# Latent attention's queries and keys split straight out of PSUM, their rows carried to the operand tiles by DMA

## The chip, the cores and the metric

The kernel runs on one core of one Trainium2 chip. The metric is the device time of one execution in microseconds (us). In the code's names nc.tensor is TensorE (PE in the profile; PEld is its weight load), nc.vector is VectorE (DVE), nc.scalar is ScalarE (ACT), nc.gpsimd is GpSimd (POOL), and nc.sync is SyncE (SP), which here only issues DMAs. PSUM is what PE writes; SBUF is the working memory.

## What is computed

The whole kernel is a decoder block: norm, one wide input projection, an indexed sparse attention (A), a latent attention (B), gates that merge them, an output projection, and a gated MLP with a convolution, on 1024 tokens of 1024 channels. The change touches latent attention, and the last gates ahead of it:

```python
q_b = einsum('bsr,rhd->bshd', c_q, w_uq)        # 8 heads, 64 plain + 32 rotary channels
q_nope, q_rope = q_b[..., :64], apply_rope(q_b[..., 64:])
k_nope = einsum('bsr,rhd->bshd', c_kv, w_uk)    # 64 per head
k_rope = apply_rope(b_kr)                       # 32, one for all heads
sc = (q_nope . k_nope + q_rope . k_rope) * (64 + 32) ** -0.5
p = softmax(where(causal, sc, -inf))
o_b = p . v_b
merged = sigmoid(g_a) * y_a + sigmoid(g_b) * y_b
```

All matrix products are made to nearly fp32 accuracy from three matmuls of split operands: each operand x is a rounded part hi and a rest lo = x - hi, and x.y is hi.hi + hi.lo + lo.hi (`mm3`, L176 to L189, and `scores`, L710).

## The kernel before

**Order of work.** `run` (L236) writes the stages down one after another; a scheduler then gives every engine one instruction list of its own, in which work that is ready on its model of time may stand ahead of work written earlier. An engine runs its list strictly in order. Around the change the text says: `prep_v` (values and the rotary part of the queries, which goes out to DRAM as `qr_d`, L1080), `prep_k(bp0, 0)` (operand tiles of the even heads, memory that had been zeroed by POOL at L1093, rotary rows of the keys at L1100 to L1103), `project(0)`, `operands(st0, 0, 0)`, the gates 14 and the first half of 15 (L323, L324), the first two score blocks, the second half of gate 15 (L331), `prep_k(bp1, 1)` (the odd heads' tiles), and `attn_b`.

**Latent attention** handles the 8 heads as 4 pairs `pr`, of an even head (`par` 0) and an odd one (`par` 1). A pair's queries and keys are projected together: 128 PSUM rows, 64 of each head. The operand tiles `hq[par]`, `hk[par]` hold hi and lo as [128, 1024] each: for an even head rows 0 to 63 are the plain channels, 64 to 95 the rotary ones, 96 to 127 zero; for an odd head the plain channels are rows 64 to 127, the rotary ones 0 to 31.

`project(pr)` (L1105) makes four PSUM tiles of 128x512 (queries and keys, two halves of the tokens), each moved to a fp32 tile `st` of the ring by ACT (L1124). `operands(st, pr, par)` (L1128) then makes, for each of the four pieces, hi by a DVE cast of 64x512 (L1136) and lo by a POOL subtraction (L1137), and copies the query's rotary rows in from `qr_d` by two DMAs on SP (L1144).

`attn_b` (L1197) has 16 steps (pr, par, j), j being the half of the eight query blocks. A step weaves three lists: the scores of its four blocks (`score_b`, matmuls L723 and the causal mask L721 into one of two PSUM tiles; minimum on DVE L1159 or L1161, exp on ACT L1167, reciprocal L1168, and scaling on POOL L1169), the `parts` (transposes L1209, hi on ACT L1218, lo on DVE L1219) and `values` (L1228) of the step before, and extra work: the next pair's `project` in step (pr, 1, 0), its even operands in (pr, 1, 1), and the odd operands in (pr+1, 0, 0). At the end of a step `finish_heads` (L1172) uses two small tiles, fin0 and fin1. All 128x512 PSUM tiles, of the projection too, come from one ring of four (`psA`). The ring `st` in SBUF has three buffers.

## Time and profile before

| | us |
|---|---|
| three timed runs | 1594.61, 1597.29, 1597.31 (median 1597.29) |
| the profiled execution, its whole time | 1594.33 |
| its span, first to last instruction | 1592.5 |
| PE busy | 1507.2 (95%) |
| DVE busy | 1187.3 (75%) |
| POOL busy | 910.5 (57%) |
| ACT busy | 789.4 (50%) |

The rows below come from this one execution; their clock starts at the span's start. A busy share is an average over stages with different limits, and a matmul's recorded length (0.39 us for 512 columns) overlaps the next one's start (0.23 us later). So the reader should go to the stretch of latent attention, about 418 to 590 us, look where PE is idle there, and see in the lists of the other engines what it waited for.

### The profile page before, as it was taken

Reading aid. Unit: us, or ns where it says so; the run is one execution under the profiler, and the core shown is the slowest. Engines: PE = TensorE matmul, PEld = TensorE weight load, DVE = VectorE, ACT = ScalarE, POOL = GpSimd, SP = SyncE. Lnnn points to the kernel's source line nnn. Section 1 sums busy time; section 2 is a strip of 40 time slices with the busy share of each in tenths; the row PEclk is TensorE's granted clock in tenths of the full one; section 3 lists DMA queues with packets and bytes.
Section 4 is the critical chain, followed back from the end, with each engine's and each line's share of the span. In section 5 each row is a group of like instructions: output and inputs, shape, how many; then the busy total and the mean of one; then the engine's idle time right before and its main releaser. Section 6 shows DMA issues by size and latency. Waiting matters only on the chain.

```text
span 1592.5 us, 21976 instructions
## 1 busy us (share of the span) xinstructions
PE 1507.2 (95%) x7586; PEld 1255.6 (79%) x7586; DVE 1187.3 (75%) x1860; ACT 789.4 (50%) x1454; POOL 910.5 (57%) x769
## 2 busy tenths in 40 slices
PE   9989999989899999999999989999999999989996
PEld 7768888867688877998878877888888887767874
DVE  7368999934588888885636668777777766896996
ACT  4545522223377788775434444444444444434445
POOL 4142122411667767654732399777777772487684
PEclk9989999999999999999999999999999999999999
DMA  7331133330300022213762132222222204964343
GB/s 256 108 105 46 54 105 97 111 115 27 106 14 17 14 83 93 76 56 118 238 198 87 53 93 80 80 80 82 81 84 84 85 36 162 329 210 127 126 137 123
DMA packets 74842, 166.25 MB, mean 104 GB/s; under 512 B 9634, under 2 KB 14114, under 8 KB 74722
## 3 DMA queue, kind: packets, MB, share of 16 engines
q1 hardware_dynamic: 62640, 139.59, 26.6%
q10 hardware_dynamic: 9490, 16.79, 2.8%
q0 software_dynamic: 2592, 8.39, 1.4%
q8 instruction: 61, 1.00, 0.3%
q14 instruction: 59, 0.48, 0.1%
HBM read 123.94 MB, written 40.53 MB: 103 GB/s over the span
## 4 chain that ended last, share of the span: by engine, by line
PE 66%; DVE 18%; issue 5%; ACT 4%; POOL 3%; DMA 3%; SPq 0%; ACTq 0%; DVEq 0%; POOLq 0%
PE tc L179 17%; PE tc L180 17%; PE tc L181 17%; PE tc L723 6%; DVE tc L155 3%; DVE tc L798 2%; DMA tc<-tc 2%; PE tc L1375 2%; PE tc L1228 2%; PE tc L1360 2%; PE tc L1209 1%; DVE tc L1136 1%; DVE tc L1002 1%; DVE tc L1159 1%; PE tc L651 1%
## 5 line engine op out<-in xcount | busy, mean ns | idle before, releaser
L179 PE MATMUL tc<-tc,tc 128*128 128x512 f32 (+2 forms) x1464 | 542.7, 374 | 9.7 <-ACT tc L1561 2.7
L181 PE MATMUL tc<-tc,tc 128*128 128x512 f32 (+2 forms) x1464 | 544.1, 372 | 4.3 <-DVE tc L155 4.3
L180 PE MATMUL tc<-tc,tc 128*128 128x512 f32 (+2 forms) x1464 | 544.3, 372 | 1.4 <-POOL tc L155 1.4
L155 POOL TENSOR_TENSOR tc<-tc,tc 128x512 fp32r<-128x512 f32 (+2 forms) x182 | 301.0, 1660 | 267.0 <-ACT tc L149 253.7
L149 ACT ACTIVATE tc<-tc 128x512 fp32r<-128x512 f32 (+1 forms) x362 | 230.5, 659 | 352.4 <-PE tc L180 242.1
L179 PEld LDWEIGHTS tc<-tc,tc 128*128 128x128 f32 x1464 | 277.3, 190 | 61.5 <-ACT tc L1561 3.0
L181 PEld LDWEIGHTS tc<-tc,tc 128*128 128x128 f32 x1464 | 277.3, 189 | 54.6 <-DVE tc L155 4.8
L180 PEld LDWEIGHTS tc<-tc,tc 128*128 128x128 f32 x1464 | 277.7, 190 | 50.5 <-POOL tc L155 2.1
L155 DVE TENSOR_TENSOR tc<-tc,tc 128x512 fp32r<-128x512 f32 x184 | 224.4, 1253 | 46.2 <-ACT tc L149 46.0
L180 PE MATMUL tc<-tc 128*128 128x512 f32 (+1 forms) x380 | 149.4, 395 | 11.6 <-DVE tc L155 11.3
L181 PE MATMUL tc<-tc 128*128 128x512 f32 (+1 forms) x380 | 146.7, 389 | 0.5 <-DVE tc L155 0.5
L179 PE MATMUL tc<-tc 128*128 128x512 f32 (+1 forms) x380 | 140.2, 389 | 1.5 <-ACT tc L149 1.2
L1169 POOL TENSOR_SCALAR tc<-tc,tc 128x128 f32<-128x128 f32 (+7 forms) x128 | 95.1, 748 | 62.2 <-DVE tc L1168 50.7
L1167 ACT ACTIVATE tc<-tc,tc 128x128 f32<-128x128 f32 (+7 forms) x128 | 96.3, 753 | 31.8 <-DVE tc L1161 13.6
L1744 DVE SCALAR_TENSOR_TENSOR tc<-tc,tc,tc 128x1023 f32<-128x1023 f32 x44 | 65.6, 1493 | 51.3 <-ACT tc L1743 51.2
L723 PE MATMUL tc<-tc 128*128 128x384 f32 (+4 forms) x352 | 89.8, 366 | 10.2 <-DVE tc L654 6.6
L180 PEld LDWEIGHTS tc<-tc 128*128 128x128 f32 x380 | 71.6, 188 | 34.8 <-DVE tc L155 20.2
L1745 DVE SCALAR_TENSOR_TENSOR tc<-tc,tc,tc 128x1022 f32<-128x1022 f32 x44 | 94.3, 2144 | 1.4
L179 PEld LDWEIGHTS tc<-tc 128*128 128x128 f32 x380 | 71.6, 189 | 17.3 <-ACT tc L149 2.2
L181 PEld LDWEIGHTS tc<-tc 128*128 128x128 f32 x380 | 71.8, 189 | 15.5 <-DVE tc L155 1.7
L723 PE MATMUL tc<-tc,tc 128*128 128x512 f32 (+4 forms) x288 | 75.2, 360 | 9.1 <-ACT tc L1167 8.2
L723 PEld LDWEIGHTS tc<-tc 128*128 128x128 f32 x352 | 60.6, 191 | 19.9 <-DVE tc L654 7.5
(266 smaller groups left out, 2429.8 us busy)
## 6 DMA issues: line engine op xcount, KB each, us to landing
tc<-tc SPq DMA_DIRECT2D x144, 256.0 KB, 3.7
tc<-in_w_up SPq DMA_DIRECT2D x44, 512.0 KB, 4.1
tc<-in_w_down SPq DMA_DIRECT2D x77, 256.0 KB, 3.7
tc<-tc ACTq DMA_DIRECT2D x52, 256.0 KB, 2.0
tc<-tc SPq DMA_DIRECT2D x20, 512.0 KB, 2.6
tc<-in_w_g SPq DMA_DIRECT2D x16, 512.0 KB, 3.6
tc<-tc POOLq DMA_DIRECT2D x24, 256.0 KB, 2.4
tc<-in_w_c SPq DMA_DIRECT2D x10, 512.0 KB, 4.4
```

The source lines that it names most:

```text
L149: self.last_split = nc.scalar.activation(hi, src, AF.Copy)
L155: e.tensor_tensor(lo, src, hi.bitcast(F32), op=OP.subtract)
L179: x = [mm(ps, lhs[0], rhs[0], start=start, stop=False, **kw), mm(ps, lhs[0], rhs[1], start=False, stop=False, **kw), mm(ps, lhs[1], rhs[0] ...
L180: mm(ps, lhs[0], rhs[1], start=False, stop=False, **kw),
L181: mm(ps, lhs[1], rhs[0], start=False, stop=stop, **kw)]
L723: self.last_score = mm(ps[:, j * 512:j * 512 + n], l, r[:, o:o + n], start=i == 0, stop=i == len(lhs) - 1)
L798: v.tensor_scalar(x, self.isc[b], c[:, j:j + 1], 0.0, op0=OP.is_ge, op1=OP.add, accum_out=cnt[:, j:j + 1])
L1167: self.last_exp = nc.scalar.activation(p3, src, AF.Exp, bias=nm, scale=-1.0, accum_out=l)
L1169: nc.gpsimd.tensor_scalar(p, p, l, 0.0, op0=OP.mult, op1=OP.add)
L1228: self.last_value = mm(po[0][:, 512 - y.shape[-1]:], lhs, y, start=kt == 0 and i == 0, stop=kt == last and i == 1, skip_group_check=True)
L1744: v.scalar_tensor_tensor(o[:, 1:], x[:, :S - 1], cw[:, t, 1:2], o[:, 1:], op0=OP.mult, op1=OP.add)
L1745: v.scalar_tensor_tensor(o[:, 2:], x[:, :S - 2], cw[:, t, 0:1], o[:, 2:], op0=OP.mult, op1=OP.add)
```

## The change

1. The gates 14 and the first half of 15 are written ahead of `prep_k`, `project(0)` and the first operands. The rotary rows of the keys become a function that runs after the projection.
2. `project` splits at once: ACT writes hi from PSUM (rounded), DVE subtracts it from PSUM for lo (scalar_tensor_tensor). For pairs 1 to 3, hi and lo are whole 128x512 pieces in `st` tiles. For pair 0 the even head's rows are written straight into the operand tiles, and the odd head's hi and lo into one `st` tile (rows 64 to 127 and 0 to 63).
3. `operands` has no DVE or POOL work any more: the 64 rows of a head go from `st` into the operand tile by one DMA of [64, 1024] for each of query hi, query lo, key hi, key lo, on SP, behind the two rotary copies (none for the even head of pair 0).
4. A fourth `st` tile comes from a pool bs of one buffer; fin0 and fin1 of latent attention have one buffer in place of two. In `prep_v` the tiles qrh and qrl are allocated first, which changes where in memory the tiles of that pool lie.

```diff
         bp0, bp0_close = self.pool("bp0", 1)
-        self.prep_k(bp0, 0)
-        self.st0, first = self.project(0)
-        for f in first + self.operands(self.st0, 0, 0):
-            f()
         self.gates(wg, go, range(MID, 15))
         self.gates(wg, go, [15], halves=(0,))
+        key_rope = self.prep_k(bp0, 0)
+        self.st0, first = self.project(0)
+        for f in first + [key_rope] + self.operands(self.st0, 0, 0):
+            f()
...
+        self.bs, bs_close = self.pool("bs", 1)
...
         pq = [self.psS() for _ in range(2)]
+        for tag in ("qrh", "qrl"):
+            self.t(tp, [P, 512], F32R, tag=tag, bufs=2)
...
+        def both(hi, lo, ps, scale):
+            nc.scalar.activation(hi, ps, AF.Copy, scale=scale)
+            v.scalar_tensor_tensor(lo, ps, scale, hi.bitcast(F32), op0=OP.mult, op1=OP.subtract)
...
+            scale = -SC_B if which == 0 else 1.0
+            if pr:
+                if hf == 0:
+                    st[which] = [self.t(self.ring, [P, S], F32R, tag="st", bufs=3) if which or k else
+                                 self.t(self.bs, [P, S], F32R, tag="st", bufs=1) for k in range(2)]
+                both(*[x[:, cs] for x in st[which]], ps, scale)
+                return
+            both(*[x[:HD, cs] for x in (self.hq, self.hk)[which][0]], ps[:HD], scale)
             if hf == 0:
-                st[which] = self.t(self.ring, [P, S], F32, tag="st", bufs=3)
-            st[which, hf] = st[which][:, cs]
-            self.nc.scalar.activation(st[which, hf], ps, AF.Copy, scale=-SC_B if which == 0 else 1.0)
+                st[which] = self.t(self.ring, [P, S], F32R, tag="st", bufs=3)
+            x = st[which]
+            nc.scalar.activation(x[HD:, cs], ps[HD:], AF.Copy, scale=scale)
+            v.scalar_tensor_tensor(x[:HD, cs], ps[HD:], scale, x[HD:, cs].bitcast(F32), op0=OP.mult, op1=OP.subtract)
...
-        def one(which, hf):
+        def one(which, k):
             rows = slice(par * HD, par * HD + HD)
-            cs = slice(hf * 512, hf * 512 + 512)
-            hi, lo = (self.hq, self.hk)[which][par]
-            nc.vector.tensor_copy(hi[rows, cs], st[which, hf][rows])
-            nc.gpsimd.tensor_tensor(lo[rows, cs], st[which, hf][rows], hi[rows, cs].bitcast(F32), op=OP.subtract)
+            x = (self.hq, self.hk)[which][par][k]
+            y = st[which][k][rows] if pr else st[which][(HD, 0)[k]:][:HD]
+            nc.sync.dma_start(x[rows].bitcast(F32), y.bitcast(F32))
...
-        return [rope] + [lambda w=w, hf=hf: one(w, hf) for hf in range(2) for w in range(2)]
+        return [rope] + [lambda w=w, k=k: one(w, k) for w in range(2) for k in range(2) if pr or par]
...
-    def finish_heads(self, pool, ps, n, par, dst):
+    def finish_heads(self, pool, ps, n, par, dst, bufs=2):
```

## Rows read from the trace of the kernel before

**Rows 1.** Page, part 4, the chain that ended last: shares by engine, by line

```profile
PE 66%; DVE 18%; issue 5%; ACT 4%; POOL 3%; DMA 3%; SPq 0%; ACTq 0%; DVEq 0%; POOLq 0%
PE tc L179 17%; PE tc L180 17%; PE tc L181 17%; PE tc L723 6%; DVE tc L155 3%; DVE tc L798 2%; DMA tc<-tc 2%; PE tc L1375 2%; PE tc L1228 2%; PE tc L1360 2%; PE tc L1209 1%; DVE tc L1136 1%; DVE tc L1002 1%; DVE tc L1159 1%; PE tc L651 1%
```

**Rows 2.** Busy time by stretch: length, each engine busy (instructions), PEclk, DMA share, GB/s

```profile
418.00:436.00 18.00, 11.08 (x54) 8.97 (x52) 11.99 (x21) 6.27 (x15) 14.29 (x15) 0.91 0.21 59
...
428.00:430.00 2.00, 2.00 (x8) 1.87 (x7) 1.10 (x2) 0.10 (x2) 2.00 (x2) 0.50 0.00 0
...
450.00:460.00 10.00, 8.12 (x48) 6.67 (x46) 9.29 (x16) 7.26 (x17) 9.81 (x10) 1.00 0.09 26
...
490.00:500.00 10.00, 8.63 (x50) 7.13 (x49) 8.93 (x17) 7.31 (x17) 9.13 (x10) 1.00 0.10 28
...
530.00:550.00 20.00, 17.52 (x106) 14.86 (x104) 17.09 (x35) 15.21 (x39) 18.16 (x25) 1.00 0.10 28
```

**Rows 3.** Timeline of PE, head: start, length, what [idle before, its releaser]

```profile
427.13 1.04 PE L723 MATMUL tc<-tc,tc 128*128 128x384 f32 x4 [3.98 <-ACT tc L1167]
...
433.82 0.36 PE L723 MATMUL tc<-tc,tc 128*128 128x256 f32 x1 [0.85 <-POOL tc L1169]
```

**Rows 4.** Timeline of DVE over the same stretch

```profile
421.10 4.45 DVE L1136 CAST tc<-tc 64x512 fp32r<-64x512 f32 x4
425.58 0.69 DVE L1161 TENSOR_REDUCE tc<-tc 128x1 f32<-128x512 f32 x1
```

**Rows 5.** Timeline of POOL over the same stretch

```profile
420.80 4.46 POOL L1093 MEMSET tc<- 32x1024 f32 x4
425.34 5.02 POOL L1137 TENSOR_TENSOR tc<-tc,tc 64x512 fp32r<-64x512 f32 x4
430.46 2.04 POOL L1169 TENSOR_SCALAR tc<-tc,tc 128x384 f32<-128x384 f32 x3
```

**Rows 6.** Groups by line, 415 to 545 us: busy, mean ns | idle before

```profile
L1136 DVE CAST tc<-tc 64x512 fp32r<-64x512 f32 x28 | 23.0, 830 | 2.2 <-ACT tc L1124 1.8
...
L1124 ACT ACTIVATE tc<-tc 128x512 f32<-128x512 f32 x12 | 7.2, 603 | 4.0 <-PE tc L181 4.0
```

**Rows 7.** Line L1032, ns min/median/max: the same subtraction, in another stage

```profile
L1032 DVE SCALAR_TENSOR_TENSOR tc<-tc,tc,tc x6: 743/743/751, 328.6 to 332.7; 128x512 fp32r<-128x512 f32 x6
```

**Rows 8.** Timeline of POOL ahead of the head

```profile
407.88 4.74 POOL L1093 MEMSET tc<- 32x1024 f32 x4 [29.45 <-DMA tc<-tc]
```

**Rows 9.** Timeline of DVE ahead of the head: the last gate half

```profile
418.13 0.69 DVE L1002 TENSOR_TENSOR tc<-tc,tc 128x512 f32<-128x512 f32 x1 [4.42 <-PE tc L181]
```

**Rows 10.** Timeline of PE, where pair 0 goes over into pair 1

```profile
454.78 0.39 PE L181 MATMUL tc<-tc 128*128 128x512 f32 x1
...
455.60 0.37 PE L723 MATMUL tc<-tc,tc 128*128 128x256 f32 x1
...
460.17 0.91 PE L1228 MATMUL tc<-tc,tc 128*128 128x512 f32 x3 [1.69 <-DVE tc L1219]
```

**Rows 11.** Timeline of DVE, same place

```profile
456.75 2.26 DVE L1136 CAST tc<-tc 64x512 fp32r<-64x512 f32 x2
...
459.45 0.67 DVE L1219 TENSOR_TENSOR tc<-tc,tc 128x512 fp32r<-128x512 f32 x1
```

**Rows 12.** Timeline of POOL, same place

```profile
458.70 2.79 POOL L1137 TENSOR_TENSOR tc<-tc,tc 64x512 fp32r<-64x512 f32 x2
461.59 1.12 POOL L1169 TENSOR_SCALAR tc<-tc,tc 128x1024 f32<-128x1024 f32 x1
```

**Rows 13.** Line L1144, rotary copies of 128 KB: issue in ns, then landing

```profile
L1144 SPq DMA_DIRECT2D tc<-tc x16: 302/364/576, 407.8 to 535.3; - x16
...
DMA to landing us min/median/max: 2.2/2.4/2.6
```

**Rows 14.** Page, part 6, DMA issues: count, KB each, median us to landing

```profile
tc<-tc SPq DMA_DIRECT2D x144, 256.0 KB, 3.7
```

**Rows 15.** Busy time, the fullest us of DMA at the head (columns as rows 2)

```profile
423.00:424.00 1.00, 0.15 (x2) 0.00 (x0) 1.00 (x2) 0.00 (x0) 1.00 (x1) 1.00 0.85 230
```

More of the change, by code (lines that the diff above doesn't have):

```diff
@@ L339, in run @@
         self.prep_k(bp1, 1)
+        self.bs, bs_close = self.pool("bs", 1)
         bt, bt_close = self.pool("bt", 1, side="right")
         before = self.attn_b(sp, bt)
+        bs_close()
         bp1_close()
@@ L1176, in finish_heads @@
         o = slice((1 - par) * HD, (1 - par) * HD + HD)
-        t0 = self.t(pool, [P, n], F32, tag="fin0", bufs=2)
-        t1 = self.t(pool, [P, n], F32, tag="fin1", bufs=2)
+        t0 = self.t(pool, [P, n], F32, tag="fin0", bufs=bufs)
+        t1 = self.t(pool, [P, n], F32, tag="fin1", bufs=bufs)
         nc.scalar.activation(t0[m, :n], ps[o], AF.Copy)
@@ L1201, in attn_b @@
         for tag in ("fin0", "fin1"):
-            self.t(bt, [P, 512], F32, tag=tag, bufs=2)
+            self.t(bt, [P, 512], F32, tag=tag, bufs=1)
         def parts(j, kt, pt, x):
@@ L1232, in values @@
                 cs = slice(j * 512, j * 512 + 512)
-                self.finish_heads(bt, po[0], 512, par, [o[m, pr, cs] for o in self.oB])
+                self.finish_heads(bt, po[0], 512, par, [o[m, pr, cs] for o in self.oB], 1)
         odd = self.operands(self.st0, 0, 1)
```

15 lines of the change are left out of this document (9 added, 6 removed).

## The prediction

> **What bounds the kernel now.** I read the page's chain first: two thirds of the chain that ended last is PE, and DVE is the only other large share [rows 1]. The line the change deletes on DVE, L1136, stands on that chain itself with 1%, some 16 us by the rounded share, so it is not hidden work everywhere. Next I read the busy time by stretch, to see where PE is not full in latent attention: 11.08 of 18 us at the head (418 to 436), 8.12 of 10, 8.63 of 10 and 17.52 of 20 at the three places where one pair of heads goes over into the next [rows 2]. That is 6.9 + 1.9 + 1.4 + 2.5 = 12.7 us of idle PE, and nearly all the change can win. Last I read the four engines' timelines at these places.
>
> At the head the reader is to see one queue. PE stands still for 3.98 us, released by an exp [rows 3]. The exp waits for the minimum of score block 3, and DVE gets to that only at 425.58, because the four casts of the odd head's operands stand ahead of it from 421.10, 4.45 us long [rows 4]; the odd head is not needed for another eight microseconds. POOL repeats the pattern: 4.46 us of memsets, then 5.02 us of subtractions, and only at 430.46 the scaling of blocks 2 to 4, without which no transposes can start [rows 5]. After the stall the granted clock is 0.50 from 428 to 430, the lower level, 1.2 GHz, and PE had been idle before it [rows 2, 3].
>
> At the first pair change PE waits 1.69 us for L1219 [rows 10], which stands behind two casts of 2.26 us [rows 11]; POOL scales the last block at 461.59, right behind two subtractions of 2.79 us [rows 12]. The other two pair changes repeat this [rows 2].
>
> **The change, part by part.** The casts: 28 lie between 415 and 545 us, 23.0 us of DVE, mean 0.83 [rows 6]; four more lie just ahead. The subtractions on POOL go too. What comes is one subtraction out of PSUM for each piece. The nearest row is L1032, same shape, source and destination: 0.743 us [rows 7]. Pairs 1 to 3 have 12 pieces, 12 x 0.743 = 8.9 us, against 24 casts, 24 x 0.83 = 19.9. So DVE is relieved by some 11 us where it is 85 to 93% busy [rows 2], besides the 4.45 us at the head. ACT's part keeps its 0.603 us for a 128x512 piece [rows 6]; in pair 0 it has two of half the rows for each.
>
> Head: with the casts gone the minimum of block 3 can run at 421.1, 4.45 us earlier [rows 4]. POOL's queue loses 5.02 us [rows 5]; its memsets stay. Both late ends move by 4.5 to 5.0 us. With the 3.98 us gap closed I also expect the half-clock stretch to go: its matmuls at full clock are 2.00 x 0.5 = 1.0 us shorter in that window alone [rows 2]. What is late next is the odd head's operands: four copies of 256 KB behind four of 128 KB, 1.5 MB, all issued from about 421. At 230 GB/s, what the fullest microsecond there moved [rows 15], that is 6.8 us, so they land near 428 to 429.5. The odd head's first score, at 433.82 now [rows 3], would come near 429: barely covered. I take **-5.5 us** for the head, bounds -3 (the copies replace part of the stall) and -7 (all idle time here).
>
> Ahead of the head: PE does the same work in another order, gates first, then projection 0, then the last gate half. That half ends at 418.1 [rows 9] and is 24 matmuls, 0.23 us apart, 5.5 us; it is the cover for the new evictions. By count these are 8 x 0.743 = 5.9 us on DVE at most, which begin with the first projected piece, 12 matmuls or 2.8 us before PE is through with the projection's 18. So the operands should be there at about 416, some 2 us before the gates end. The memsets there waited 29.45 us for a DMA [rows 8], the writing out of qrh and qrl; these are now first in their pool, so that the operand tiles lie over others; without that the direct evictions would wait until 407.9, and the gates ahead cover even this. On SP the two rotary copies, issued at 407.8 [rows 13], move behind the first half of gate 15's store; they slip to about 409 and land (2.4 us [rows 13]) before 412. I take **+0.4 us**, bounds -1 and +4 (the score blocks wait for all evictions with no cover).
>
> Pair changes: gain and price in one place. Gain: the 1.69 us wait and smaller ones, up to the idle time, 1.9, 1.4 and 2.5 us. Price: today a score block starts 0.43 us after the projection's last matmul (454.78 + 0.39 = 455.17 to 455.60 [rows 10]), as its 256 columns need the first token half alone. Now a copy carries a whole row, so every score waits for the last piece: 0.60 ACT + 0.74 DVE + 0.36 issue + landing. No row shows a 64-row copy of 256 KB. Below it is the rotary copy, half the bytes, 2.4 us [rows 13]; above it stands the 256 KB group with 3.7 [rows 14]. I take 2.4 plus another 128 KB at 230 GB/s, 0.6: 3.0, nearest to the rotary copy, which has the same row length. Together 4.7 us: scores start at 459.9, 4.3 later than now. What covers this: the transposes and value matmuls of the two odd-head steps still to do, 36 transposes and 24 value matmuls. They wait today for DVE and for POOL's scaling at 461.59; without the 2.79 us of subtractions ahead the scaling ends by 459.9 [rows 12], and the minimum and exp ahead of it move up by the casts in their way. So I see PE filled until the copies land, but the lead that the scores had is gone. I take **-1.3 us** for each of three, -3.9; bounds -2.4 (all its idle time goes) and +3.1.
>
> The Trainium skill, SBUF — State Buffer, section "Door 1: The DMA port swizzle (why `[64,N]` ≈ `[32,N]`)", speaks against these copies: 64 rows reach 8 of the 16 ports, about 218 GB/s behind a fixed 2 us or so. By it 256 KB is an estimated 3.2 us, and two key copies together 4.4; the sum would be some 0.5 us worse at each change, 7.5 us of gain in place of 9.0. The rate agrees with the 32-row copies here [rows 15].
>
> Other waits. SP now stands in front of copies that wait for DVE's evictions and for the last score that reads the tile; behind them stand later rotary copies and, in the last pair, the loads of attention A's keys, which run ahead of their use; I take nothing, and late ones count in the +3.1. The four-tile PSUM ring is held about 0.74 us longer by each projected piece, since DVE reads it after ACT: up to 3 us a pair if the transposes need the slot, else nothing; inside the bounds above. fin0 and fin1 with one buffer: used once a step, roughly every 10 us, and the reader on POOL is freed of the subtractions: nothing.
>
> Sum: -5.5 + 0.4 - 3.9 = **-9.0 us**. Against the profiled execution (1594.33: span 1592.5, 1.8 around it) that is 1585.3. Two of the three timed runs are 3 us above it, and the median is 1597.29; carried over, 1588.3, called **1588**.
>
> **The rivals.** (a) The copies take back the pair changes. If 4.3 us of lost lead costs as much as the casts gave, +1.3 each: -5.5 + 0.4 + 3.9 = -1.2, 1596. For it: ACT is at 7.3 of 10 us there and DVE at 9 [rows 2], so late scores can't be caught up at once. Against it: PE had idle time because of the very queues that are emptied. (b) Slower: the engine lists put the next pair's scores ahead of the transposes, and PE stands at them until the copies have landed. With 3.7 us of landing [rows 14] and the second copy behind the first, 0.7, the scores start 455.17 + 0.60 + 0.74 + 0.36 + 4.4 = 461.3, 5.7 later than now; less the 1.9 us that PE idles there anyway, +3.8 each, 11.4 for three. With the head at -5.5 and +0.4 that gives +6.3, 1603.6. It decides from about +2.8 us a pair change on. For it: a list is fixed before the run, by a model of the copy's time. Against: PE has nothing to lose by doing transposes first. (c) The head does not gain: the odd head's copies land after 431, or POOL's memsets keep the scaling late, -1 in place of -5.5: 1592.8, still faster.
>
> **How the numbers follow.** About 0.2%, 3.2 us, is what a measurement of this kernel can tell from no change. Chances: the forecast 0.60, (c) 0.08, (a) 0.17, (b) 0.15. Faster 0.68, same 0.17, slower 0.15. Range: downward the bounds allow -7 - 1 - 7.2 = -15 us, 1582, and from the lower level of the timed runs 3 less, 1579; upward it takes in (c) and (a) to 1598 and leaves out (b).
>
> **What would show it.** Right: no casts and no subtractions; DVE's minimum of block 3 directly behind that of block 2; the gap of 3.98 us gone and PEclk 1.00 throughout; POOL's scaling following the memsets; PE's idle time before L1228 at the pair changes under 0.5 us; copies of 256 KB that land in about 3 us. Wrong: PE waiting before L723 for a DMA, or SP's copies issued late; waits for a PSUM slot ahead of the projection; first scores later than 418. The forecast falls if pair changes still show 2 us of idle PE, then by DMA.

## The result, and the profile of the changed kernel

The changed kernel takes 1604.35 us, median of 5 runs (1601.96 to 1610.18), against 1596.56 for the kernel before in the same comparison: a ratio of 1.0054, 95% interval 1.0031 to 1.0078. It is slower by 0.5%, where 1588 had been forecast. The profiled execution is 1604.7, with a span of 1602.9, 10.4 us longer than before.

The engines were relieved as foreseen: the casts and subtractions are gone, DVE's busy time falls from 1187.3 to 1174.3 us and POOL's from 910.5 to 866.6. The chain by engine and by line (page, part 4; before: [rows 1]) says who took their place:

```profile
PE 63%; DVE 16%; DMA 6%; issue 5%; ACT 5%; POOL 3%; SPq 1%; ACTq 0%; DVEq 0%; POOLq 0%
PE tc L180 17%; PE tc L181 16%; PE tc L179 16%; PE tc L725 6%; DMA tc<-tc 4%; DVE tc L800 2%; DVE tc L155 2%; PE tc L1397 2%; PE tc L1250 2%; PE tc L1382 1%; PE tc L1231 1%; DVE tc L1004 1%; ACT tc L149 1%; POOL tc L155 1%; DVE tc L749 1%
```

DVE goes from 18 to 16%, DMA from 3 to 6%. PE lost share too, although it does the same work: it is waiting for something that it did not wait for before.

To see where, I set six marks on PE's and DVE's timelines, the same events in every kernel: the DVE product of the last gate half, the first matmul (L179) of projections 1, 2 and 3, the last value matmul of latent attention (B) and the last row of value matmuls of attention A. All times are from the profiled executions, in us; the rows of the experiments below stand in the same table, and are read when their turn comes.

| kernel | gate half at | gate half to proj. 1 | proj. 1 to 2 | proj. 2 to 3 | proj. 3 to end of B | end of B to end of A | span |
|---|---|---|---|---|---|---|---|
| before | 418.1 | 23.7 | 39.9 | 40.5 | 68.6 | 153.3 | 1592.5 |
| after | 421.6 | 17.4 | 41.5 | 43.7 | 77.4 | 154.8 | 1602.9 |
| e1_pair0 | 419.8 | 18.8 | 43.6 | 40.5 | 68.6 | 153.4 | 1591.2 |
| e2_pairs | 419.3 | 23.7 | 39.7 | 43.8 | 76.1 | 157.5 | 1609.2 |
| e3_order | 419.8 | 18.8 | 39.1 | 40.1 | 76.0 | 156.3 | 1595.2 |
| e4_direct | 422.7 | 17.5 | 42.1 | 40.3 | 72.5 | 153.4 | 1590.2 |
| e5_own | 421.2 | 17.5 | 42.0 | 40.3 | 68.9 | 158.8 | 1593.7 |
| e6_order14 | 419.8 | 17.3 | 39.2 | 41.3 | 76.9 | 154.5 | 1594.5 |
| e8_gates | 417.2 | 24.4 | 39.9 | 40.5 | 68.3 | 153.4 | 1592.1 |
| e9_halves | 419.2 | 18.8 | 39.4 | 38.1 | 74.6 | 158.5 | 1595.6 |
| e10_both | 419.6 | 17.3 | 39.4 | 38.1 | 71.7 | 157.1 | 1587.2 |
| e11_pair0_own | 421.2 | 18.8 | 43.5 | 40.5 | 69.4 | 157.0 | 1597.6 |
| e12_warm | 421.4 | 15.9 | 40.0 | 38.2 | 70.0 | 156.5 | 1586.4 |
| e13_early | 421.0 | 16.0 | 39.9 | 38.1 | 69.1 | 157.6 | 1587.7 |
| e14_pair0_warm | 420.5 | 15.9 | 42.6 | 41.8 | 67.9 | 153.3 | 1586.1 |

Of after: the gate half comes 3.5 us later, 2.3 of which were there by 375 us, in a stage whose code is the same; the head gains 6.3; then the pairs lose 1.6, 3.2 and 8.8, and attention A 1.5. The rest of the span gives 1.9 back. That sums to the 10.4 us.

The head, PE's timeline (start, length, what, idle before it and its releaser; before: [rows 3]):

```profile
432.98 0.36 PE L725 MATMUL tc<-tc,tc 128*128 128x256 f32 x1 [2.15 <-issue]
434.12 0.80 PE L725 MATMUL tc<-tc,tc 128*128 128x256 f32 x2 [0.67 <-DMA tc<-tc]
```

The stall of 3.98 us ahead of block 3 is gone. What PE waits for now is the odd head's rows, 2.15 and 0.67 us. The first row names no releaser, but the copy of the odd keys' high part lands at 432.78, 0.20 us before it, and in every other kernel with these copies the same score starts 0.20 to 0.24 us behind that landing; the second wait ends with the landing of the low part.

The first pair change, PE's timeline (before: [rows 10]):

```profile
453.94 0.40 PE L181 MATMUL tc<-tc 128*128 128x512 f32 x1
...
457.33 0.90 PE L1250 MATMUL tc<-tc,tc 128*128 128x512 f32 x3 [0.90 <-DVE tc L1241]
459.71 0.39 PE L725 MATMUL tc<-tc,tc 128*128 128x256 f32 x1 [1.48 <-DMA tc<-tc]
...
460.96 1.12 PE L725 MATMUL tc<-tc,tc 128*128 128x256 f32 x4 [0.40 <-DMA tc<-tc]
```

The old wait for DVE shrank from 1.69 to 0.90 us, and two waits for copies came, 1.48 and 0.40. Line L725 is the score; the transposes (L1231) of the last odd-head step stand behind it in PE's list, although POOL had scaled the last of their input by 457.55. No run puts them first, so what another list would be worth is not shown. The other two changes show 1.15 and 1.49, and 1.14 and 1.57.

Busy time by stretch (length, busy us of each engine with its instructions, granted clock, DMA share, GB/s; before: [rows 2]):

```profile
434.00:436.00 2.00, 1.88 (x6) 1.58 (x7) 1.04 (x4) 0.46 (x2) 0.38 (x2) 0.50 0.05 8
450.00:460.00 10.00, 7.25 (x40) 5.60 (x39) 7.18 (x14) 6.75 (x14) 5.07 (x8) 1.00 0.75 173
458.00:460.00 2.00, 0.52 (x4) 0.29 (x3) 0.68 (x2) 0.55 (x1) 1.56 (x3) 1.00 1.01 231
460.00:462.00 2.00, 1.60 (x10) 1.37 (x10) 0.31 (x2) 0.28 (x1) 0.00 (x0) 0.77 0.97 205
462.00:464.00 2.00, 2.00 (x11) 2.00 (x11) 0.84 (x4) 1.46 (x5) 0.85 (x2) 0.50 0.03 4
464.00:466.00 2.00, 2.00 (x15) 1.96 (x14) 1.43 (x3) 1.48 (x4) 0.00 (x0) 0.87 0.00 0
530.00:550.00 20.00, 17.10 (x92) 14.63 (x91) 13.02 (x28) 11.68 (x28) 7.50 (x12) 0.91 0.55 126
```

Read the first column of counts and the clock together. From 450 to 460 DVE is down to 7.18 of 10 us and POOL to 5.07, as intended, and PE is busy 7.25 where it was 8.12. At 458 to 460 it has 0.52 us of work, DMA moves 231 GB/s, and after that the granted clock is 0.50, the lower level (1.2 GHz). The same work then takes longer, and this counts as busy: the sum of PE's busy time times the missing clock, from 410 to 606 us in pieces of 2 us, is 9.5 us here against 1.7 before, while PE's idle time there is about the same, 19.0 against 20.4.

Last, SP's timeline at the first pair change:

```profile
447.87 1.19 SPq L1159 DMA_DIRECT2D tc<-tc  x2
452.97 0.77 SPq L1166 DMA_DIRECT2D tc<-tc  x2
453.80 5.48 SPq L1159 DMA_DIRECT2D tc<-tc  x6
```

and the line of all such copies (issue in ns, min, median and max, then landing; the nearest rows of before are [rows 13, 14]):

```profile
L1159 SPq DMA_DIRECT2D tc<-tc x28: 461/662/1238, 426.8 to 545.1; - x28
...
DMA to landing us min/median/max: 2.9/4.1/6.1
```

By the program's SP list, the two copies at 447.87 are the even head's queries. The rotary pair at 452.97 and the first two of the six at 453.80 are for the **odd** head, which is needed two steps later; the even head's keys, which the next score waits for, are third and fourth, issued at 455.00 and 455.85. The chain of waits there (start, length, what) goes through the last of these:

```profile
454.87 0.95 ACT tc L1189
455.82 0.03 issue
455.85 5.07 DMA tc<-tc
460.92 0.04 issue
460.96 1.12 PE tc L725 x4
```

### The profile page after: what moved, and what is told of

Its sections match the earlier page's. It is cut to its first block, busy times and chain, and to the rows that moved or that the text cites. A ratio compares the mean times of both kernels' runs of the same rounds, so it can differ in the third digit from the quotient of the medians.

```text
span 1602.9 us, 22009 instructions
## 1 busy us (share of the span) xinstructions
PE 1518.1 (95%) x7586; PEld 1265.5 (79%) x7586; DVE 1174.3 (73%) x1848; ACT 791.8 (49%) x1458; POOL 866.6 (54%) x737
## 4 chain that ended last, share of the span: by engine, by line
PE 63%; DVE 16%; DMA 6%; issue 5%; ACT 5%; POOL 3%; SPq 1%; ACTq 0%; DVEq 0%; POOLq 0%
PE tc L180 17%; PE tc L181 16%; PE tc L179 16%; PE tc L725 6%; DMA tc<-tc 4%; DVE tc L800 2%; DVE tc L155 2%; PE tc L1397 2%; PE tc L1250 2%; PE tc L1382 1%; PE tc L1231 1%; DVE tc L1004 1%; ACT tc L149 1%; POOL tc L155 1%; DVE tc L749 1%
## 5 line engine op out<-in xcount | busy, mean ns | idle before, releaser
L179 PE MATMUL tc<-tc,tc 128*128 128x512 f32 (+2 forms) x1464 | 543.6, 374 | 11.1 <-ACT tc L1583 2.8
L179 PEld LDWEIGHTS tc<-tc,tc 128*128 128x128 f32 x1464 | 277.6, 190 | 63.3 <-ACT tc L610 3.2
L179 PE MATMUL tc<-tc 128*128 128x512 f32 (+1 forms) x380 | 140.3, 387 | 3.1 <-ACT tc L149 3.0
L725 PE MATMUL tc<-tc 128*128 128x384 f32 (+4 forms) x352 | 89.2, 364 | 9.7 <-DVE tc L656 6.3
L180 PEld LDWEIGHTS tc<-tc 128*128 128x128 f32 x380 | 72.1, 190 | 31.2 <-DVE tc L155 15.9
L725 PE MATMUL tc<-tc,tc 128*128 128x512 f32 (+4 forms) x288 | 76.4, 369 | 11.0 <-DMA tc<-tc 5.6
L179 PEld LDWEIGHTS tc<-tc 128*128 128x128 f32 x380 | 71.7, 189 | 18.5 <-ACT tc L149 3.6
L725 PEld LDWEIGHTS tc<-tc 128*128 128x128 f32 x352 | 60.6, 191 | 19.8 <-DVE tc L656 7.3
```

The costliest lines, as they stand in the source:

```text
L179: x = [mm(ps, lhs[0], rhs[0], start=start, stop=False, **kw), mm(ps, lhs[0], rhs[1], start=False, stop=False, **kw), mm(ps, lhs[1], rhs[0] ...
L180: mm(ps, lhs[0], rhs[1], start=False, stop=False, **kw),
L725: self.last_score = mm(ps[:, j * 512:j * 512 + n], l, r[:, o:o + n], start=i == 0, stop=i == len(lhs) - 1)
```

## The experiments

Three questions: which part of the change costs, what at a pair change costs it, and what happens in the last pair, which loses most. Ratios are against the kernel before, each from runs on one chip, with a 95% interval; the chip is not the same for all of them, so kernels are compared by ratio. The theory at the start was that the copies at the pair changes, not the head, are at fault, through their place on SP's queue; its rivals are written with each run.

**e1_pair0 and e2_pairs: one part each.** e1 keeps the new order at the head and pair 0's new form, and gives pairs 1 to 3 the old form; e2 is the other half.

Against the changed kernel, e1 (operands likewise):

```diff
             if pr:
                 if hf == 0:
-                    st[which] = [self.t(self.ring, [P, S], F32R, tag="st", bufs=3) if which or k else
-                                 self.t(self.bs, [P, S], F32R, tag="st", bufs=1) for k in range(2)]
-                both(*[x[:, cs] for x in st[which]], ps, scale)
+                    st[which] = self.t(self.ring, [P, S], F32, tag="st", bufs=3)
+                st[which, hf] = st[which][:, cs]
+                nc.scalar.activation(st[which, hf], ps, AF.Copy, scale=scale)
                 return
```

Against the kernel before, e2 (its copies as in the change):

```diff
+            if pr:
+                if hf == 0:
+                    st[which] = [self.t(self.ring, [P, S], F32R, tag="st", bufs=3) if which or k else
+                                 self.t(self.bs, [P, S], F32R, tag="st", bufs=1) for k in range(2)]
+                hi, lo = [x[:, cs] for x in st[which]]
+                self.nc.scalar.activation(hi, ps, AF.Copy, scale=scale)
+                self.nc.vector.scalar_tensor_tensor(lo, ps, scale, hi.bitcast(F32), op0=OP.mult, op1=OP.subtract)
+                return
```

> Only the part for pair 0: gates first, pair 0 split straight out of PSUM, its odd head's rows by DMA; pairs 1 to 3 keep the fp32 tile, the DVE casts and the POOL subtractions of before, and fin0 and fin1 their two buffers. Theory L (the loss is at the pair changes, where scores wait for copied rows and TensorE then runs at half clock): the head keeps its gain, from the end of the last gate half to projection 1's first matmul 17.4 us as in the changed kernel against 23.7 in the kernel before, and the pair changes are as before, PE waiting 1.7 us for DVE there; total 1590 to 1593. Rival H (the new order ahead of the head and the odd rows of pair 0 by DMA cost what was lost): total 1600 or more. Rival R (the loss comes from ring buffers and the single fin buffers, spread over the stage): total near 1592 as well, so this run does not tell R from L.

> Only the part for pairs 1 to 3: split out of PSUM into whole tiles, rows of both heads by DMA, the pool bs and the single fin buffers; gates, pair 0 and its casts as before. Theory L: the head shows the 4 us gap of before, and each of the three pair changes shows waits of scores for a DMA of 1 us or more and a stretch of granted clock near 0.5; total 1607 to 1612. Rival H: total as before or less, 1590 to 1597.

Measured: e1 1590.91, ratio 0.9971 (0.9956 to 0.9986); e2 1611.53, ratio 1.0097 (1.0074 to 1.0120). The change is two changes of opposite sign: one of some -4.6 us, one of some +15. In e1's table row everything from projection 2 on is as before, but of the 4.9 us that its head gains only 1.2 are left there (62.4 against 63.6 us from the gate half): projection 1 to 2 takes 3.7 us longer. A granted clock of 0.50 for 3.4 us from 459 explains at most 1.7 of these; the rest is open. In e2's the head is as before, to the tenth, and the loss is in projection 2 to 3, the last pair and attention A.

**e3_order: the odd copies behind the even ones.**

```diff
+            return self.tc.issue_after(self.last_copy.ins) if pr and par else ExitStack()
...
-            nc.sync.dma_start(x[rows].bitcast(F32), y.bitcast(F32))
+            with behind():
+                i = nc.sync.dma_start(x[rows].bitcast(F32), y.bitcast(F32))
+            if pr and not par:
+                self.last_copy = i
```

> The changed kernel with one edit: on SP the odd head's six copies of a pair are held behind the even head's four, where the changed kernel issued the odd queries' copies ahead of the even keys'. Theory L in its narrow form (the even keys' copies are late because odd copies stand in line ahead of them): the even keys land about 3 us after issue in place of 5, waits of scores for a DMA at the three changes fall from 1.5 us and more to under 0.7, the half-clock stretches shorten; total 1593 to 1599. Rival W (the whole-row copy is late by itself, through eviction, issue and landing, whatever stands in line): scores still wait about 1 us and more, the clock still falls; total 1600 to 1604.

Measured: 1597.56, ratio 1.0015 (1.0000 to 1.0031), from 1.0054 (1.0031 to 1.0078): the place in the queue was worth about 6 us, by intervals that just meet. PE's timeline:

```profile
457.48 0.39 PE L725 MATMUL tc<-tc,tc 128*128 128x256 f32 x1 [1.52 <-DMA tc<-tc]
...
537.69 0.38 PE L725 MATMUL tc<-tc,tc 128*128 128x256 f32 x1 [1.84 <-DMA tc<-tc]
549.92 0.49 PE L1257 MATMUL tc<-tc,tc 128*128 128x512 f32 x1 [2.90 <-ACT tc L1247]
```

The second wait is gone, the score comes 4.5 us after the projection's last L179 (453.00) where after has 6.2 (453.48 to 459.71), and the two middle columns of the table fall to 39.1 and 40.1, below before. What got shorter is the landing, not the way to the issue: the even keys' first copy goes out 1.5 us behind the last L179 in both kernels (at 455.00 in after, at 454.50 in e3), but lands after 2.93 us instead of 4.67, and the second after 3.70 instead of 5.07. In after the odd queries' copies were still under way then, the first of them until 456.95. But a wait of 1.5 to 1.9 us for a copy stays at each change, as rival W had it, and the last pair stays at 76.0; there PE waits 2.90 us for a cast, which is no copy. So the queue's order is one cause of three.

**e9_halves: the even copies cut in two.** A score block of the first token half needs 512 columns alone; so each even copy of e3 becomes two of 128 KB. Against e3:

```diff
-                i = nc.sync.dma_start(x[rows].bitcast(F32), y.bitcast(F32))
+                i = nc.sync.dma_start(x[rows, cs].bitcast(F32), y[:, cs].bitcast(F32))
...
+        if pr and not par:
+            return [rope] + [lambda w=w, k=k, c=c: one(w, k, slice(512 * c, 512 * c + 512))
+                             for c in range(2) for w in range(2) for k in range(2)]
```

> The changed kernel with the odd rows' copies behind the even ones on SyncE's queue, and each even copy of pairs 1 to 3 cut into two transfers, one for each half of the tokens (128 KB each). Theory W (what is left at a pair change is a copy that must wait for the last projection although the first scores read the first half alone): TensorE's waits for a copy at the three changes (1.52, 1.91 and 1.84 us) fall under 0.5 and the time from 1597.6 to about 1592. Rival X (the copies are bound by the DMA engines they share with each other, or by their issue): the waits stay at 1.3 to 2 us and the time at 1597 or more.

Measured: 1594.70, ratio 1.0002 (0.9989 to 1.0016); about 2 us better than e3, where 5 had been expected. PE's timeline at the first and last pair change and behind it:

```profile
457.20 0.91 PE L1260 MATMUL tc<-tc,tc 128*128 128x512 f32 x3 [0.47 <-DVE tc L1251]
...
533.44 0.91 PE L1260 MATMUL tc<-tc,tc 128*128 128x512 f32 x3 [0.46 <-DVE tc L1251]
543.91 1.11 PE L1241 MATMUL tc<-tc,tc 128*128 128x128 f32 x4 [3.13 <-DVE tc L1212]
```

and ACT's and DVE's ahead of the last line:

```profile
541.93 0.31 ACT L1317 ACTIVATE tc<-tc 128x128 fp32r<-128x128 f32 x1 [3.68 <-DMA tc<-tc]
...
542.47 0.59 ACT L1211 ACTIVATE tc<-tc 64x512 f32<-64x512 f32 x1
543.16 0.69 DVE L1212 TENSOR_TENSOR tc<-tc,tc 64x512 f32<-64x512 f32 x1 [4.18 <-ACT tc L1211]
```

The waits for copies are gone at all three changes, and only 0.47 us for DVE is left: the pair change that the prediction had forecast. Projection 2 to 3 takes 38.1 us, 2.4 less than before, and projection 1 to 2 takes 39.4, 0.5 less. As e9 keeps the pool bs and the single fin buffers, rival R of e1 is not what costs at the pair changes. What eats the gain is the last pair (74.6 against 68.6): ACT stands 3.68 us at a load of attention A's keys. Behind it in ACT's list stands the copy that begins to empty a PSUM tile at the end of a step (L1211, then L1212 on DVE); PE waits 3.13 us for that and then runs at the lower clock (0.50 from 544 to 550). And attention A is 5 us longer, with a granted clock of 0.50 from 602 to 608.

**e4_direct: no even copies at all.** Every pair in pair 0's form: even rows straight from PSUM into the operand tiles, odd rows by copy.

```diff
-            if pr:
...
-                both(*[x[:, cs] for x in st[which]], ps, scale)
-                return
```

> All pairs in the form that the change gives to pair 0: the even head's rows are written from PSUM straight into the operand tiles, only the odd head's go through a tile and four DMAs; no pool bs, two fin buffers. It costs 4 more ACT and 4 more DVE instructions of 64x512 a pair (0.6 and 0.69 us each) than whole pieces do. Theory L, narrow form or W: no score waits for an even row by DMA, the clock stays up at the pair changes, the head keeps its gain; total 1586 to 1592. Rival R (PSUM tiles held longer by evictions in two steps on ACT and DVE): pair changes lose on waits for DVE or ACT in place of DMA; total 1598 or more.

Measured: 1591.72, ratio 0.9981 (0.9966 to 0.9995). At the pair changes PE waits 0.79 us for ACT and for no copy. This supports the copies of even rows as the cost of the pair changes from another side. The last pair is long again, 72.5.

**e5_own, e6_order14, e10_both, e13_early: the last pair.** The key loads of attention A share three buffers with the projections' rows, and the odd copies hold these until they have landed; in before the first load was issued at 515.7 us, in e3 at 542.8. Theory P: the buffers make the loads late, and ACT, in its order, stands at them. e5 adds buffers for the loads to e4; e6 starts the stage one step later in e3; e10 adds buffers to e9.

e5 against e4:

```diff
-            raw = self.t(self.ring, [P, S], F32, tag="st", bufs=3)
+            raw = self.t(self.bs, [P, 512], F32, tag="pa", bufs=2)
```

e6 against e3:

```diff
-PREP_A = 13
+PREP_A = 14
```

e10 against e9 (the GpSimd copy goes into a second such tile):

```diff
-            raw = self.t(self.ring, [P, S], F32, tag="st", bufs=3)
+            raw = self.t(sp, [P, 256], F32, tag="pS", bufs=8)
```

> All four pairs in pair 0's form (even rows straight from PSUM, odd rows by transfer, as in the run with that alone), and attention A's eight key loads get two buffers of their own instead of three shared with the projections' rows. Theory P (the loads come late because their buffers are held until the odd copies have landed, and ScalarE, which takes its work in order, stands at them with the operand casts behind it): the first load is issued before 520 us instead of 537, the last pair (projection 3's first matmul to the last value matmul) falls from 72.4 us to about 69, and the time from 1591.7 to about 1588. Rival R (the last pair loses its time to the odd copies and to the clock behind short waits, and the loads are hidden): the last pair stays at 72 and the time at 1591 to 1592.

> The changed kernel with the odd rows' copies behind the even ones on SyncE's queue, and the preparation of attention A (key loads, their casts and transposes) begun one of the 16 steps later, in the 15th instead of the 14th. Theory P: ScalarE no longer stands 2.45 us at a load that has not landed, TensorE's 2.90 us wait for the cast behind it and the half clock after it go, the last pair falls from 76.0 us to about 71 and the time from 1597.6 to about 1593. Rival R: the last pair stays near 76, because the waits are for copies, and the time at 1597 to 1598. If the five parts that now crowd into each of the last two steps cost more than the wait, the last pair gets longer than 76.

> The kernel with ordered, halved even copies, and attention A's eight key loads moved from the three buffers that they shared with the projections' rows to small score buffers of 256 columns (8 of them, which stand free by then). Theory P (in the last pair ScalarE stands 3.68 us at a key load that came late because the odd copies held its buffer, with the operand casts behind it, TensorE waits 3.13 us and then runs at half clock for 8 us): the wait and the half clock behind it go, projection 3's first matmul to the last value matmul falls from 74.6 us to about 68, and the time by 5 to 6 us against the run without this edit, to 0.997 of the kernel before. Rival G (attention A's first queries, copied by GpSimd, are ready at a time of their own): the last value matmul comes 5 us sooner, but TensorE waits for GpSimd ahead of attention A's first transposes about as much longer, and the time stays within 2 us.

Measured: e5 1596.64, 1.0018 (1.0003 to 1.0034), worse than e4; e6 1598.18, 1.0027 (1.0015 to 1.0039), no better than e3, although ACT's waits for the loads fall from 4.6 to 1.8 us (the last pair is 76.9); e10 1591.92, 0.9988 (0.9975 to 1.0001), better than e9 by about 2 us where 5 to 6 were expected, with intervals that overlap. In the last pair e5 did what P said, 72.5 to 68.9, but it lost 5.4 us in attention A. Its first two loads went out at 420 us, ahead of all copies of pairs 1 to 3, so it does not tell the buffers from the place on SP. In e10 the buffers did a part: the first load goes out at 536.01 instead of 538.85, and the last pair is 71.7 instead of 74.6. SP's timeline in the last pair:

```profile
517.10 13.70 SPq L1163 DMA_DIRECT2D tc<-tc  x8
530.89 1.00 SPq L1173 DMA_DIRECT2D tc<-tc  x2
531.94 3.97 SPq L1163 DMA_DIRECT2D tc<-tc  x4
536.01 1.27 SPq L1307 DMA_DIRECT2D tc<-tc  x1
```

ACT's:

```profile
540.21 0.31 ACT L1318 ACTIVATE tc<-tc 128x128 fp32r<-128x128 f32 x1 [3.02 <-DMA tc<-tc]
```

and PE's:

```profile
542.00 0.50 PE L1260 MATMUL tc<-tc,tc 128*128 128x512 f32 x1 [2.28 <-ACT tc L1250]
```

SP stands 13.7 us at the eight halves, goes through the odd copies, and only then, at 536.01, issues the first load (L1307): ACT waits 3.02 us and PE 2.28. It is not the buffer that holds it: e13, below, issues three loads into the same buffers at 508. Theory P had the right waiter and, for this kernel, no more than a part of the cause. Theory Q: the load is late because of its place on SP. e13 issues the first three loads ahead of pair 3's copies (on top of e12, below, which shows ACT's wait too, 2.37 us):

```diff
+            if n == 11:
+                extra = [lambda b=b: self.load_a(b) for b in range(3)] + extra
```

> The kernel with ordered, halved even copies, small buffers for the key loads and the twelve repeats at the head, and now the first three of attention A's eight key loads issued on SyncE's queue ahead of pair 3's copies instead of behind them. Theory Q (the load is late because it stands in SyncE's queue behind copies that wait for their operand tiles; a buffer of its own did not help, ScalarE still waited 2.4 to 3.0 us at it): ScalarE's wait for the load near 540 us and TensorE's 1.6 to 2.3 us wait for the cast behind it go, projection 3's first matmul to the last value matmul falls from 69.7 us to about 66, and the time falls by 2 to 4 us against the run without this edit (0.9965 of the kernel before), to about 0.994. Rival R (the loads' ScalarE work is bound by something else, such as the GpSimd copy or the transposes): the last pair stays at 69 to 70 and the time within 1 us.

Measured: 1588.20, 0.9958 (0.9943 to 0.9974), against 0.9965 for e12: no difference that the intervals tell apart. SP's timeline:

```profile
508.37 1.31 SPq L1309 DMA_DIRECT2D tc<-tc  x3
...
535.93 1.25 SPq L1309 DMA_DIRECT2D tc<-tc  x1
```

and ACT's:

```profile
526.15 0.30 ACT L1327 ACTIVATE tc<-tc 128x128 fp32r<-128x128 f32 x1
...
540.08 0.31 ACT L1327 ACTIVATE tc<-tc 128x128 fp32r<-128x128 f32 x1 [2.25 <-DMA tc<-tc]
```

The three early loads are used at 526 to 530 us without a wait; the fourth, still behind the copies, is issued at 535.93 and ACT waits 2.25 us at it. So a load ahead of the copies costs no wait and one behind them does; but to move three of eight only passed the wait on to the next, and the last pair is 69.1 instead of 70.0 (69.7 in the expectation, which took the row that holds the last matmul). The time that Q named was not gained here.

**e11_pair0_own: the price of the small buffers.** e1 with e10's edit of the buffers alone (the same lines).

> Pair 0 alone in the new form (pairs 1 to 3 as before), with attention A's key loads in small score buffers of their own. Control for theory P: here the loads were issued at about 516 us, long before they are needed, and the last pair took 68.6 us as before, so the edit changes nothing: last pair 68 to 69 us, time as without it, 0.997 of the kernel before. If the small buffers are worth something by themselves (fewer waits on the shared ones), the time falls by 1 us or more.

Measured: 1597.10, 1.0012 (1.0000 to 1.0024), where e1 had 0.9971: the edit costs some 6 us by the two ratios, and nothing had been expected. Little changes up to the end of B (69.4 against 68.6); attention A takes 157.0 instead of 153.4. PE's timeline there:

```profile
603.17 0.44 PE L1389 MATMUL tc<-tc,tc 128*128 128x128 f32 x2 [2.09 <-POOL tc L1197]
```

and the busy time by stretch:

```profile
602.00:604.00 2.00, 0.44 (x2) 0.20 (x2) 0.54 (x3) 1.26 (x3) 1.83 (x3) 0.91 0.18 19
604.00:606.00 2.00, 1.47 (x5) 1.18 (x6) 1.67 (x3) 1.03 (x3) 1.99 (x2) 0.50 0.37 120
```

With the edit the work on POOL at the start of attention A comes in another order; PE waits 2.09 us for a scaling instead of 1.24 for the queries, and then runs at 0.50 for some 7 us. The same loss stands in the rows of e5, e10, e12 and e13. That the order on POOL is what starts it is what the timelines suggest; no run changes it alone. e9 and e3, which have no such edit, lose there as well, in their profiled executions, each behind waits for POOL of 1.1 and 0.6 us; after has the same two waits (1.09 and 0.58) without a fall of the clock there.

**e8_gates: the order at the head alone**, in the kernel before.

```diff
+        self.gates(wg, go, range(MID, 15))
+        self.gates(wg, go, [15], halves=(0,))
         self.prep_k(bp0, 0)
...
-        self.gates(wg, go, range(MID, 15))
-        self.gates(wg, go, [15], halves=(0,))
```

> The kernel before with one change: the last gates' lines stand ahead of the key preparation and the first projection, as in the changed kernel; the queries and keys are still cast by VectorE and subtracted by GpSimd. Theory S (the head gains because pair 0's operands come straight out of PSUM, in 0.7 us pieces instead of four casts of 4.45 us and subtractions of 5 us): the wait of about 4 us for GpSimd ahead of the first scores stays or grows, since the casts now stand behind the last gates, and the time is 1595 to 1599. Rival O (the order alone brings the gain): the time is about 1591, as with pair 0 alone in the new form.

Measured: 1595.63, 1.0015 (0.9997 to 1.0032), with the stall still in PE's timeline:

```profile
426.37 1.65 PE L723 MATMUL tc<-tc,tc 128*128 128x384 f32 x4 [4.00 <-ACT tc L1167]
```

The order alone brings nothing; the gain at the head comes from pair 0's operands straight out of PSUM, as theory S had it.

**e12_warm and e14_pair0_warm: the price of the clock.** At the head PE waits about 2 us for the odd head's rows, and the granted clock is 0.50 after that. Twelve repeats of one transpose, with the same result, fill the wait; e12 has them on top of e10, e14 on top of e1.

```diff
+                for _ in range(13 if pt is self.pt0 and (j, kt, qb) == (0, 2, 3) else 1):
+                    nc.tensor.transpose(pp[:, (qb - q0) * P:(qb - q0 + 1) * P], pt[qb][:, kt * P:(kt + 1) * P], self.ident)
```

> The kernel with ordered, halved even copies and the key loads in small buffers, and at the head TensorE repeats one transpose twelve times (same result) right before the first score of head 1, where it waits about 2.2 us for the odd copies and then runs at half clock for 5 to 8 us. Theory C (the half clock follows from the idle stretch, and costs as much as the wait): with the engine busy through the wait the granted clock stays at 1.00 from 428 to 440 us, projection 1's first matmul comes 2 to 3 us sooner, and the time falls by 2 to 3 us against the run without the repeats. Rival D (the stretch is bound by the other engines, or the clock falls later instead): projection 1 begins within 1 us of where it did, and the time is the same.

> Pair 0 alone in the new form, pairs 1 to 3 as before, and TensorE repeats one transpose twelve times right before the first score of head 1, through the 2.19 us in which it waits for the odd copies. Theory C (the half clock after that wait costs 2 to 4 us): the granted clock stays near 1.00 from 428 to 440 us instead of 0.50 for some 8 us, projection 1's first matmul comes 3 us sooner after the last gate half than 18.8 us, and the time falls from 0.997 of the kernel before to about 0.995. Rival D (the gain seen with the repeats on the other kernel came from the reordering of its other instructions): the time stays at 0.997.

Measured: e12 1588.15, 0.9965 (0.9954 to 0.9976), where e10 had 0.9988; e14 1587.37, 0.9952 (0.9937 to 0.9968), where e1 had 0.9971. Busy time by stretch, first of e1:

```profile
430.00:432.00 2.00, 0.55 (x2) 0.30 (x2) 0.63 (x2) 1.24 (x3) 1.02 (x1) 0.87 1.02 203
432.00:434.00 2.00, 1.68 (x6) 1.38 (x7) 0.85 (x3) 0.46 (x2) 0.21 (x1) 0.50 0.15 31
436.00:438.00 2.00, 2.00 (x10) 2.00 (x9) 0.42 (x2) 0.42 (x2) 0.48 (x1) 0.50 0.00 0
```

and of e14:

```profile
430.00:432.00 2.00, 1.14 (x11) 0.93 (x10) 1.77 (x4) 1.86 (x5) 1.01 (x1) 1.00 1.02 199
432.00:434.00 2.00, 1.34 (x8) 1.00 (x9) 0.43 (x3) 0.16 (x1) 0.18 (x1) 1.00 0.51 98
436.00:438.00 2.00, 2.00 (x15) 1.70 (x13) 0.79 (x3) 0.99 (x4) 0.81 (x2) 1.00 0.00 0
```

With the twelve transposes in the stretch of the wait the clock stays at 1.00, 15 matmuls instead of 10 lie in the 2 us from 436, and projection 1 begins 15.9 us after the gate half instead of 18.8: 2.9 us, as expected. By the ratios it is 3.0 us on e1, with intervals that overlap, and 3.7 on e10, which was timed together with e12. On e12 the other instructions moved a little too; on e14 the first odd score comes 11.4 us behind the gate half, as in e1 (431.89 - 420.47, 431.23 - 419.80), so the 2.9 us lie behind the wait, some 0.2 of them for one value matmul that now follows projection 1's first. The lower clock is thus shown as a cost of its own, about as large as the wait that precedes it.

The table shows the same price without the repeats. Behind the same wait, 2.15 to 2.33 us, the granted clock is 0.50 for 6.8 us in e1, e3, e9 and e11 and for 3.4 us in after, e4, e5, e6 and e10. From the gate half to projection 1 the first four take 18.8 us and the other five 17.3 to 17.5; the three kernels with the repeats, in which it does not fall there, take 15.9 to 16.0.

**e14 has the lowest ratio of the study**, which the intervals do not tell from e13's; it is 7.3 us below before by the medians of its comparison and keeps of the change what pair 0 does.

## Why the prediction was wrong

**The head was right in the main.** Forecast -5.5 with bounds of -3 and -7; measured 6.3 from the gate half to projection 1, part of which is given back by projection 2 (from the gate half to there 59.0 against 63.6 us, 4.6, with the first pair change in it). e1, which has this part alone, gains 4.9 at the head and keeps 1.2 of it to projection 2 in its profiled execution; by its ratio it gains 4.6 (2.2 to 7.0). The order of the pieces was right as well: DVE's casts and POOL's subtractions had to go, and the odd rows are what is late next. "Barely covered" was optimistic: the first odd score waits 2.15 us and its second part 0.67 more. Of the clock it was wrong: the half-clock stretch did not go with the stall, it followed the new wait (0.50 from 434 to 436, 0.70 to 438). Its price is some 1.5 us where it lasts 3.4 us, as in after, and 2.9 where it lasts 6.8, as in e1 (17.4 and 18.8 against 15.9).

**Ahead of the head** +0.4 with an upper bound of +4 was forecast. The gate half is 3.5 us late, but 2.3 of that were there by 375 us, 2.0 of them from a stretch with the lower clock before 340 us, which is some 7 us long in before (322 to 329), some 10 in after, and one or the other in each of the other kernels, with the same code. What is left is 1.2, inside the bounds. As such a stretch can add some 2 us to any one profiled execution, the table's spans are weaker evidence than the ratios.

**The failed step is the pair change**, -1.3 us each, -3.9 in all; e2, which has it alone, is some 15 us slower than before. It failed in three terms.

First, the start of the scores. Forecast: 4.7 us after the projection's last matmul. Measured at the first change: from 454.34 to 459.71, 5.4, for the first matmul, and to 460.96, 6.6, for the one that needs the low part. The landing was taken at 3.0 and is 4.1 by the median of the 21 copies whose landing the trace has, 5.07 for the copy that PE waited for. The Trainium skill, SBUF — State Buffer, gives the rate in its section "Door 1: The DMA port swizzle (why `[64,N]` ≈ `[32,N]`)" and the fixed 2 us in "The DMA setup-cost knee (why "@ 1 MiB" ≠ asymptote)"; from them the prediction drew an estimate of 3.2 us a copy and 4.4 for two. The trace of e3 bears this out: its first key copy lands after 2.9 to 3.0 us, and the two together took 4.4 at the first and the third change (454.50 to 458.92, 534.65 to 539.09). In after they took 5.9, from the first issue (455.00) to the last landing (460.92), behind the two odd copies, which neither figure contained. So 3.0 fits one copy with nothing ahead of it, but the score needs two, and here two more stood ahead. (That two cost only some 0.5 us a change more, as the prediction says beside the estimate, does not follow: 4.4 is 1.4 above 3.0.) With e3's order the score starts 1.7 us sooner behind the projection and the ratio falls by 0.4%. The prediction had named SP's queue, but only what stands behind the copies, not the order among them.

Second, the cover. "So I see PE filled until the copies land" is the sentence that fell. PE ran out of work at 458.2, about 1.5 us before the first copy had landed and with scores ahead of the transposes in its list, which is rival (b)'s mechanism as far as a timeline can show it. e9, where no score waits for a copy, shows what the gain would have been: projection 2 to 3 takes 2.4 us less than before and projection 1 to 2 takes 0.5 less, against 1.3 forecast for each. So the casts were worth about what the sum said.

Third, what follows a wait. The sum had no term for a clock that falls behind PE's idle time, although the profile of before shows one behind its 3.98 us [rows 2, 3]. After has the lower clock behind all three changes and again at 570 to 574: 9.5 us of missing clock from 410 to 606, against 1.7. Idle time itself did not grow. Of the 10.4 us between the profiled executions these 7.8 are the largest part that can be counted, as an estimate: not every matmul at the lower clock need have delayed what follows.

**The last pair** was the line "I take nothing": the loads of attention A's keys behind the copies on SP. In e9 they hold ACT for 3.68 us and PE for 3.13, and the last pair loses 6.0 us, twice what the pairs before it gain (2.9). In after itself the first load is 30 us later than before, and ACT waits for the loads 2.8 us in all; how much of its 8.8 us in the last pair they make, next to the copies, was not separated.

Rival (b) gave 1603.6, and the median is 1604.35. Its mechanism is what PE's list shows, but that the sums agree is partly luck: it priced three equal changes at 3.8 us each, and measured are 1.6, 3.2 and 8.8, the last with another cause in it, and a clock term that it did not have. Its chance of 0.15 was too small: the argument against it, that PE loses nothing by doing transposes first, was about what could be listed, when the row to look for was what the list would hold.

One bound of the sum was too wide by the prediction's own rows: -2.4 us for each change "(all its idle time goes)" is about the third window's idle time, not that of the other two (1.9 and 1.4), and with -7 for the head it makes 14.2 us of gain where 12.7 of idle PE had been found. It did not decide anything.

What stays open: what e1 loses between projections 1 and 2, what moves POOL's order at the start of attention A in the kernels that lose 4 to 5 us there, and whether all eight loads ahead of the copies would bring e13's last pair to the 66 us that were expected. The last two were not tried alone.

## What to carry to other kernels

A copy between tiles that replaces work on two engines is paid for at the first instruction that needs it: find that instruction in the trace, count what PE has left to do before it, and compare that with issue, landing and every transfer that stands ahead on the same queue, needed or not. Move a piece that the consumer can use by itself (half a row) rather than the whole, and keep transfers that nobody needs yet, and waits on an operand tile, behind those that somebody waits for. Where the trace shows the lower clock behind an idle stretch of PE, count that stretch twice: once for the wait, and once for the matmuls behind it. At the head a wait of some 2.2 us cost up to 2.9 us more in this way.

## What the runs showed of the hardware

The granted clock fell to 0.50 behind stretches in which PE had little to do, such as 1.30 busy us of 4 (430 to 434 us of after) or 0.87 (540 to 544 of e9), and stayed there for some 3.4 or 6.8 us (up to 10 ahead of the head) although PE was fully busy again for most of it; twelve small transposes in such a stretch kept it at 1.00. The same engine work, in the same place, met this in one kernel and not in another: e1 fell to 0.50 behind the wait of 1.62 us at the first pair change, which before has too (1.69) without a fall.

Copies of 64 rows by 1024 columns landed in 2.9 us at best, in 4.1 us by the median of the 21 (of 28) whose landing the trace of after has, and in up to 6.1 when several were in flight and DMA moved 205 to 238 GB/s; of the 40 copies of e10, 24 of which have half as long a row, the median of the 30 known is 2.3. On SP an issue of such a copy took 0.46 us at the least, 0.66 by the median and up to 1.24, against 0.36 for the 32-row rotary copies of before [rows 13].
